# Where softmax is normalised in the sparse mixer of a two-layer hybrid decoder

## The chip, the cores and the metric

The kernel runs on one core of a Trainium2 chip. The metric is the device time of one execution in microseconds (us). The kernel before takes 1989.84 us, the median of three runs (1989.49, 1989.84 and 1992.78 us). A trace of one profiled execution stands beside these times.

A core has a matrix engine (TensorE, PE in the profile, with its weight loads as PEld), a vector engine (VectorE, DVE), a scalar engine (ScalarE, ACT), GpSimd (POOL) and a queue engine (SyncE, SP) that only starts transfers here. Each engine works through its own queue of instructions in order and waits on semaphores for the others. In this kernel the matrix engine writes its results to PSUM tiles and reads its operands from SBUF tiles.

## The reference

Each of two layers computes three token mixers from one input projection, merges them with per-channel gates, and adds a SwiGLU block. The sequence has 512 tokens, the model 1024 channels. The change is in the sparse mixer A, with 8 heads of 64 channels in 2 groups. It has three branches, each an attention of its own, and sums them with a sigmoid gate for each head, token and branch:

```
q_r = rope(q, pos)
s   = einsum(q_r, k_sel) * scale ;  p   = masked_softmax(s,   causal)     # selected blocks
s_w = einsum(q_r, k_win) * scale ;  p_w = masked_softmax(s_w, causal)     # sliding window
o_s = einsum(p, v_sel) ;  o_w = einsum(p_w, v_win)
o_c = einsum(masked_softmax(compressed scores), v_cmp)
g   = sigmoid(gate_logits)                      # 3 gates per head and token
o   = g[0] * o_c + g[1] * o_s + g[2] * o_w
```

With 512 tokens and 16 selected blocks of 64, and a window of 512, the selected and the window branch are both full causal attention, each with its own keys and values. Mixer B (multi-head latent attention, also 8 heads) runs through the same code without gates.

## The kernel before, in words

Each float32 product is made of three passes: an operand is split into a rounded part and a remainder (`split`, lines 98 to 100: the scalar engine copies, the vector engine or GpSimd subtracts), and `mm3` issues three matmuls.

The attention of a layer is a list of 24 jobs: 16 for mixer A (8 heads, and for each head branch b = 0, selected, and b = 1, window) and then 8 for mixer B. `attn` walks through slots g, three for each job, and in each slot issues one third of a stage for several jobs at once, so that the stages of different jobs overlap:

- `st_s` in slots 0 to 2 of a job: the score matmuls into a PSUM tile `pss` (two buffers, tag "s"); the masked row minimum `nm` on the vector engine (line 632); the exponential on the scalar engine into `P` in SBUF, with the row sum as a second result (line 635).
- `st_n`, four slots after a job's first: normalising, on the vector engine. For mixer A it takes the reciprocal of the row sums (line 642) and multiplies each of the job's four tiles `P` by the gate and by the reciprocal (line 644). For mixer B it only takes the reciprocal, for two heads at once (line 646).
- `st_t`, six slots after: `P` is transposed on the matrix engine (line 659) into a PSUM tile `pst` (three buffers, tag "t") and split into two tiles (line 100 on the scalar, line 101 on the vector engine).
- `st_v`, eight slots after: the product with the values into the PSUM tile `pso` (one buffer, tag "o", lines 672 and 673). For mixer A both branches of a head accumulate into the same tile: the first branch starts the accumulation (`first`), the second closes it (`last`). Only then is `pso` copied out: one half by the scalar engine (line 681), and the vector engine adds the other half to it (line 682). An even head fills the upper half of the tile `od`, an odd head the lower half.

After an odd head of mixer A the compressed branch is computed in one matmul (line 687) and added (line 688), and the sum is split into the operands of the projection that follows. After an odd head of mixer B the reciprocals are broadcast along 64 columns by the scalar engine (line 691), transposed on the matrix engine into a `pst` tile (line 696), and multiplied onto `od` (line 697). So mixer B normalises after the product with the values, on transposed outputs of two heads, and mixer A before it.

Between the stages `fill` issues matmuls of projections from a list (`fillers`) at a rate worked out from their due slots, and `step` issues small vector or GpSimd work from a list (`bg`: rotary embedding and norms of queries and keys). This order of issue is the program order. The tile framework then puts each engine's queue in an order of its own from dependencies, priorities and a model of durations; weight loads have a raised priority (`WPRI`). In the attention of both layers GpSimd makes the remainder of the weights (`wl`, line 101) and of the outputs (`oT`, `cq`), since `weng` is GpSimd there.

The tiles `od` and the broadcast `lb` come from the pool tag "e", with three buffers, which many other steps use too.

Of the kernel before, what the change touches and what calls it, by code (L numbers as in the profile page):

```python
# [12 lines left out]
F32R = mybir.dt.float32r  # L13
I32 = mybir.dt.int32
AF = mybir.ActivationFunctionType
# [48 lines left out]
class Builder:  # L64
    def __init__(self, ctx, tc, io, layers=L, dbg=None):
        self.tc, self.nc, self.io, self.layers = tc, tc.nc, io, layers
        self.dbg = dbg or {}
        nc = self.nc
        self.V, self.A, self.T = nc.vector, nc.scalar, nc.tensor
        pool = lambda n, b=1, **k: ctx.enter_context(tc.tile_pool(name=n, bufs=b, **k))  # L70
        self.cst, self.sb, self.sm = pool("cst"), pool("sb"), pool("sm", 2)
        self.psum = pool("psum", 1, space=PSUM)
        self.n = 0
        self.bufs = dict(wr=3, wh=4, wl=4, h=16, mg=8, oT=8, cq=10, qk=8, v=8, big=6, pt=5, P0=2, P1=2, P2=2, P3=3, e=3)
        self.pending = False
        self.pbufs = dict(mm=2, s=2, t=3, o=1)
        self.wide, self.turn = False, 0
        self.weng, self.debt, self.mid = None, 0.0, False

# [13 lines left out]
    def small(self, shape, tag, dt=F32):  # L93
        return self.sm.tile(shape, dt, tag=tag, name=self.nm(tag), bufs=2 if tag in ("vec", "nm", "l", "lp") else 1)
# [520 lines left out]
    def st_s(self, j, s):  # L615
        if s == 0:
            j.Pi = [self.pg(f"P{i}", F32, [128, 128 * i + 128]) for i in range(NT)]
            j.nm = self.small([128, NT], "nm")
            if j.cmp:
                j.l = self.small([128, NT], "l")  # L620
            else:
                if j.h % 2 == 0:
                    self.lp = self.small([128, 2, NT], "lp")
                j.lp = self.lp
                j.l = j.lp[:, j.h % 2]
# [12 lines left out]
    def st_n(self, j, part):  # L638
        V = self.V
        if j.cmp:  # L640
# [24 lines left out]
    def st_v(self, j, s):  # L665
        T = self.T
        if j.first and s == 0:
            self.o = self.ps("o")
        o = self.o
        for kt in ((0,), (1,), (2, 3))[s]:  # L670
            h, l_, m0, n = j.dst[kt]
            T.matmul(o[:, 512 - n:], j.V[kt], h[:, m0:m0 + n], start=j.first and kt == 0, stop=False)  # L672
            T.matmul(o[:, 512 - n:], j.V[kt], l_[:, m0:m0 + n], start=False, stop=j.last and kt == NT - 1)  # L673
        if s < 2:
            return
        if j.last:
            odd = j.h % 2
            if not odd:
                self.od = self.pg("e")
            r, s = (slice(64, 128), slice(0, 64)) if odd else (slice(0, 64), slice(64, 128))  # L680
            self.A.activation(self.od[r], o[s], AF.Copy)
            self.V.tensor_tensor(self.od[r], o[r], self.od[r], OP.add)
            if odd:
                if j.cmp:
                    pc = self.ps("t")
                    r = slice((j.h // 2 % 2) * 64, (j.h // 2 % 2) * 64 + 64)
                    T.matmul(pc, self.vbd[j.h // 4][r], self.PcT[r], start=True, stop=True)
                    self.V.tensor_tensor(self.od, pc, self.od, OP.add)
                else:
                    lb = self.pg("e")  # L690
                    self.A.activation(lb.rearrange("p (i h d) -> p i h d", i=NT, h=2),
                                      j.lp.rearrange("p h i -> p i h")[:, :, :, None].to_broadcast([128, NT, 2, 64]),
                                      AF.Copy)
                    pc = self.ps("t")
                    for i in range(NT):
                        T.transpose(pc[:, i * 128:i * 128 + 128], lb[:, i * 128:i * 128 + 128], self.ident)
                    self.V.tensor_tensor(self.od, pc, self.od, OP.mult)
                if j.cmp:
                    hi, lo = self.pg("oT", F32R), self.pg("oT", F32R)
                else:  # L700
                    hi, lo = self.pg("cq", F32R), self.pg("cq", F32R)
                self.split(hi, lo, self.od, self.weng)
                self.yo.append((hi, lo))
# [29 lines left out]
    def a_jobs(self, g):  # L733
        jobs = []
        for h in range(4 * g, 4 * g + 4):
            for b in range(2):
                j = Job()
                j.h, j.first, j.last, j.cmp = h, b == 0, b == 1, True

                def op(j=j, h=h, b=b):  # L740
                    k1, k2 = self.Kt[b]
                    q = self.Qt[h % 4]
                    j.gate = self.gth[:, :, h * 3 + 1 + b]
# [170 lines left out]
    def b_jobs(self):  # L914
        jobs = []
        for h in range(B_H):
            j = Job()
            j.h, j.first, j.last, j.cmp, j.gate = h, True, True, False, None
# [385 lines left out]
def build(d, layers=L, dbg=None):  # L1304
    nc = bacc.Bacc("TRN2", target_bir_lowering=False, num_devices=1)
# [18 lines left out]
```

## Time and profile before

| | |
|---|---|
| median of three runs | 1989.84 us (1989.49 to 1992.78) |
| span of the profiled execution | 1990.7 us; the page lists no longer time for it |
| PE busy | 1942.9 us, 98% |
| PEld busy | 1638.4 us, 82% |
| DVE busy | 1317.9 us, 66% |
| ACT busy | 996.6 us, 50% |
| POOL busy | 251.0 us, 13% |
| mean granted TensorE clock | 0.991 |

The jobs of mixer A run from about 115 to 312 us of the span in the first layer and from about 1100 to 1292 us in the second. Busy time is the time in which an engine had an instruction at work. The ends of matmuls are modelled, and neighbours overlap, so the start of the next matmul tells more of its real cost than its duration. A granted clock of 1.00 is 2.4 GHz and 0.50 is 1.2 GHz; a value between is a stretch with both.

### The profile page before, as it was taken

How to read it: one execution, taken by the hardware profiler on the slowest of the kernel's cores; microseconds unless marked ns; L12 is line 12 of the kernel's file. 1: busy time of each engine (PE TensorE's matmuls, PEld its weight loads, DVE VectorE, ACT ScalarE, POOL GpSimd, SP SyncE). 2: the span in 40 equal slices, each digit the busy share in tenths (PEclk: the TensorE clock that was granted, in tenths of full speed). 3: DMA queues.
4: the chain of work that ended last, by engine and by line, in shares of the span. 5: the costliest groups of instructions: out<-in, count | busy, mean ns of one | idle time of the engine just before them, and what ended most of it. 6: DMA issues, size and time to landing. Idle time of an engine off the chain costs nothing.

```text
span 1990.7 us, 26971 instructions
## 1 busy us (share of the span) xinstructions
PE 1942.9 (98%) x9472; PEld 1638.4 (82%) x9472; DVE 1317.9 (66%) x2783; ACT 996.6 (50%) x1937; POOL 251.0 (13%) x232
## 2 busy tenths in 40 slices
PE   9899999999999999999998899999999999999999
PEld 8878878888888888888888688888888888888887
DVE  8689998788545554455555999977884455534552
ACT  5456776687334332233344577767773343323331
POOL 0453442000000000000004535410000000000000
PEclk9898999999999999999999999999999999999999
DMA  5221111233333333333432111113333323333333
GB/s 155 76 68 30 38 33 42 89 93 101 111 122 101 95 96 97 99 95 98 130 113 87 48 37 47 33 47 98 96 102 116 122 95 96 95 97 99 96 102 99
DMA packets 100519, 173.94 MB, mean 87 GB/s; under 512 B 11936, under 2 KB 26144, under 8 KB 100384
## 3 DMA queue, kind: packets, MB, share of 16 engines
q1 hardware_dynamic: 100384, 172.22, 28.3%
q8 instruction: 74, 1.21, 0.3%
q14 instruction: 61, 0.50, 0.1%
HBM read 167.98 MB, written 4.19 MB: 86 GB/s over the span
## 4 chain that ended last, share of the span: by engine, by line
PE 79%; DVE 7%; ACT 2%; issue 1%; ACTq 0%; DVEq 0%
PE pst L113 10%; PE pst L115 10%; PE pst L114 10%; PE psmm L113 8%; PE psmm L114 8%; PE psmm L115 8%; PE pss L114 7%; PE pss L113 7%; PE pss L115 7%; PE pst L659 2%; DVE P L644 1%; DVE pss L632 1%; PE pso L672 1%; PE pso L673 1%; PE pst L543 1%
## 5 line engine op out<-in xcount | busy, mean ns | idle before, releaser
L100 ACT ACTIVATE wh<-wr 128x512 fp32r<-128x512 f32 (+3 forms) x640 | 387.7, 608 | 705.3 <-PE pst L114 261.3
L101 DVE TENSOR_TENSOR wl<-wr,wh 128x512 fp32r<-128x512 f32 (+2 forms) x526 | 355.0, 676 | 249.5 <-ACT wh L100 244.5
L101 POOL TENSOR_TENSOR wl<-wr,wh 128x512 fp32r<-128x512 f32 (+2 forms) x114 | 137.9, 1215 | 962.8 <-ACT wh L100 951.4
L113 PE MATMUL psmm<-h,wh 128*128 128x512 f32 x600 | 237.8, 396 | 1.4 <-ACT wh L100 1.0
L114 PE MATMUL psmm<-h,wh 128*128 128x512 f32 x600 | 235.6, 393 | 0.0
L115 PE MATMUL psmm<-h,wl 128*128 128x512 f32 x600 | 235.2, 392 | 0.0
L113 PE MATMUL pst<-h,wh 128*128 128x512 f32 x512 | 199.7, 390 | 0.0
L115 PE MATMUL pst<-h,wl 128*128 128x512 f32 x512 | 199.2, 389 | 0.0
L114 PE MATMUL pst<-h,wh 128*128 128x512 f32 x512 | 199.2, 389 | 0.0
L113 PE MATMUL pss<-h,wh 128*128 128x512 f32 x344 | 134.1, 390 | 0.0
L115 PE MATMUL pss<-h,wl 128*128 128x512 f32 x344 | 133.9, 389 | 0.0
L114 PE MATMUL pss<-h,wh 128*128 128x512 f32 x344 | 133.8, 389 | 0.0
L113 PEld LDWEIGHTS psmm<-h,wh 128*128 128x128 f32 x600 | 113.5, 189 | 23.7 <-ACT wh L100 1.3
L115 PEld LDWEIGHTS psmm<-h,wl 128*128 128x128 f32 x600 | 113.4, 189 | 23.6
L114 PEld LDWEIGHTS psmm<-h,wh 128*128 128x128 f32 x600 | 113.6, 189 | 20.9
L635 ACT ACTIVATE P<-pss,nm 128x512 f32<-128x512 f32 x192 | 100.1, 525 | 55.4 <-DVE nm L632 32.3
L113 PEld LDWEIGHTS pst<-h,wh 128*128 128x128 f32 x512 | 96.1, 188 | 20.2 <-ACT e L983 0.4
L115 PEld LDWEIGHTS pst<-h,wl 128*128 128x128 f32 x512 | 96.1, 188 | 20.0
L114 PEld LDWEIGHTS pst<-h,wh 128*128 128x128 f32 x512 | 96.1, 188 | 19.8
L632 DVE CUSTOM_DVE_ANT_0 pss<-pss,mask 128x512 f32<-128x512 f32 x192 | 93.9, 490 | 7.5 <-PE pss L115 6.4
L659 PE MATMUL pst<-ident,P 128*128 128x128 f32 x480 | 77.8, 277 | 9.0 <-DVE P L644 5.3
L659 PEld LDWEIGHTS pst<-ident,P 128*128 128x128 f32 x480 | 59.3, 143 | 25.3 <-issue 15.0
(419 smaller groups left out, 4316.3 us busy)
## 6 DMA issues: line engine op xcount, KB each, us to landing
wr<-w SPq DMA_DIRECT2D x240, 256.0 KB, 2.6
wr<-wfm SPq DMA_DIRECT2D x188, 256.0 KB, 2.7
wr<-wpc SPq DMA_DIRECT2D x32, 256.0 KB, 2.7
wr<-wo SPq DMA_DIRECT2D x32, 256.0 KB, 2.6
wr<-wb SPq DMA_DIRECT2D x32, 192.0 KB, 2.4
wr<-w SPq DMA_DIRECT2D x32, 192.0 KB, 2.3
mg<-xT SPq DMA_DIRECT2D x16, 256.0 KB, 2.8
wr<-wpa SPq DMA_DIRECT2D x16, 256.0 KB, 2.6
```

What stands on the lines that cost most here:

```text
L100: self.A.activation(hi, src, AF.Copy)
L101: (eng or self.V).tensor_tensor(lo, src, hi.bitcast(F32), OP.subtract)
L113: mm(ps, a[0], b[0], start=first, stop=False)
L114: mm(ps, a[0], b[1], start=False, stop=False)
L115: mm(ps, a[1], b[0], start=False, stop=last)
L543: self.T.transpose(ps[:w, i * 128:i * 128 + 128], src(i, slice(c0, c0 + w)), self.ident)
L632: self.V.tensor_tensor_reduce(p[:, :W], p[:, :W], self.mask[:, 512 - W:], 1.0, 3e38, OP.add, OP.min, j.nm[:, i:i + 1])
L635: self.A.activation(j.Pi[i], p[:, :128 * (i + 1)], AF.Exp, bias=j.nm[:, i:i + 1], scale=-1.0, accum_out=j.l[:, i:i + 1])
L644: V.tensor_scalar(j.Pi[i], j.Pi[i], j.gate[:, i:i + 1], j.l[:, i:i + 1], op0=OP.mult, op1=OP.mult)
L659: self.T.transpose(ps[:, c:c + 128], j.Pi[i][:, kt * 128:kt * 128 + 128], self.ident)
L672: T.matmul(o[:, 512 - n:], j.V[kt], h[:, m0:m0 + n], start=j.first and kt == 0, stop=False)
L673: T.matmul(o[:, 512 - n:], j.V[kt], l_[:, m0:m0 + n], start=False, stop=j.last and kt == NT - 1)
```

## The change

For mixer A the probabilities are no longer scaled. Each branch gets its own `pso` tile, from its start to its end, and is copied out by itself into a tile `od` of its own (tag "od", three buffers). After an odd head, for each branch, the reciprocals of both heads are multiplied by the gates (one product of 128x8), broadcast by the scalar engine, transposed on the matrix engine, and multiplied onto the branch's `od`, as mixer B did already. After the second branch GpSimd adds the two branches, and then the compressed branch is added as before. The row sums of two heads share a tile for each branch (`lp0`, `lp1`). The scratch space for descriptors of dynamic transfers is set to 1024, which leaves SBUF for the three new buffers.

```
-self.bufs = dict(..., P3=3, e=3)
+self.bufs = dict(..., P3=3, e=3, od=3)
...
 def st_n(self, j, part):
-    if j.cmp:
-        a = 2 - 2 * part
-        V.reciprocal(j.l[:, a:a + 2], j.l[:, a:a + 2])
-        for i in (a + 1, a):
-            V.tensor_scalar(j.Pi[i], j.Pi[i], j.gate[:, i:i + 1], j.l[:, i:i + 1], op0=OP.mult, op1=OP.mult)
-    elif j.h % 2 and part:
+    if j.h % 2 and part:
         V.reciprocal(j.lp, j.lp)
+        if j.cmp:
+            V.tensor_tensor(j.lp, j.lp, j.gate, OP.mult)
...
 def st_v(self, j, s):
-    if j.first and s == 0:
+    if s == 0:
         self.o = self.ps("o")
...
+    odd = j.h % 2
+    if not odd:
+        self.od[j.b] = self.pg("od")
+    od = self.od[j.b]
     r, s = (slice(64, 128), slice(0, 64)) if odd else (slice(0, 64), slice(64, 128))
+    self.A.activation(od[r], o[s], AF.Copy)
+    self.V.tensor_tensor(od[r], o[r], od[r], OP.add)
+    if not odd:
+        return
+    lb = self.pg("e")
+    self.A.activation(lb.rearrange(...), j.lp.rearrange(...).to_broadcast([128, NT, 2, 64]), AF.Copy)
+    pc = self.ps("t")
+    for i in range(NT):
+        T.transpose(pc[:, i * 128:i * 128 + 128], lb[:, i * 128:i * 128 + 128], self.ident)
+    self.V.tensor_tensor(od, pc, od, OP.mult)
+    if j.cmp and j.b == 0:
+        return
+    if j.cmp:
+        o0 = self.od[0]
+        self.weng.tensor_tensor(od, od, o0, OP.add)
+        pc = self.ps("t")
+        T.matmul(pc, self.vbd[j.h // 4][r], self.PcT[r], start=True, stop=True)
+        self.V.tensor_tensor(od, pc, od, OP.add)
...
-    nc = bacc.Bacc("TRN2", target_bir_lowering=False, num_devices=1)
+    nc = bacc.Bacc("TRN2", target_bir_lowering=False, num_devices=1, dynamic_dma_scratch_size=1024)
```

The whole program loses 128 scalings of `P` and 64 reciprocals of 128x2 on the vector engine. It gains there 16 reciprocals of 128x8, 16 products of 128x8, 16 additions of 64x512 and 16 products of 128x512; 64 transposes on the matrix engine; 16 copies of 64x512 and 16 broadcasts of 128x512 on the scalar engine; and 8 additions of 128x512 on GpSimd. No transfer is added or removed.

The first place is the vector engine's queue in the first layer, where the second and third jobs of mixer A stand; before, with `P` the probabilities, `l` the row sums and `gth` the gates:

```order
L604 TENSOR_TENSOR e_1517<-e_1517,cl_1546 128x16x31
L642 RECIPROCAL l_1498<-l_1498 128x2 x2
L101 TENSOR_TENSOR pt_1640<-pst_1641,pt_1639 128x384
L644 TENSOR_SCALAR P_1496<-P_1496,gth_830,l_1498 128x512
L644 TENSOR_SCALAR P_1495<-P_1495,gth_830,l_1498 128x384
L644 TENSOR_SCALAR P_1494<-P_1494,gth_830,l_1498 128x256
L644 TENSOR_SCALAR P_1493<-P_1493,gth_830,l_1498 128x128
L632 ISA pss_1647,nm_1610<-pss_1647,mask 128x384
L632 ISA nm_1610 128x1
```

The same place now, where `lp` are the row sums of two heads:

```order
L605 TENSOR_TENSOR e_1510<-e_1510,cl_1533 128x16x31
L102 TENSOR_TENSOR pt_1585<-pst_1586,pt_1584 128x512
L340 TENSOR_TENSOR mg_1609<-psmm_1497,rsb_469 128x512
L639 RECIPROCAL lp_1316<-lp_1316 128x8
L677 TENSOR_TENSOR od_1619<-pso_1581,od_1619 64x512
L641 TENSOR_TENSOR lp_1316<-lp_1316,gth_830 128x8
L102 TENSOR_TENSOR pt_1625<-pst_1626,pt_1624 128x384
L630 ISA pss_1632,nm_1597<-pss_1632,mask 128x384
L630 ISA nm_1597 128x1
```

The four scalings that stood between the split of a transpose (`pt`) and the next row minimum (`nm`) are gone; the copy of a branch out of `pso` and the two small operations on `lp` stand there.

The second place is the end of the second pair of heads in the first layer. On the vector engine before, where `e_2303` is the tile `od` of both branches:

```order
L821 TENSOR_REDUCE bss_2557<-e_2569 128x4
L158 SCALAR_TENSOR_TENSOR bkt_2477<-bkt_2477,bks_2435 128x8
L682 TENSOR_TENSOR e_2303<-pso_2409,e_2303 64x512
L159 SCALAR_TENSOR_TENSOR bky_2476<-bkt_2477,bky_2476 128x8
L644 TENSOR_SCALAR P_2421<-P_2421,gth_830,l_2426 128x128
L688 TENSOR_TENSOR e_2303<-pst_2582,e_2303 128x512
```

And now, where `od_2291` is the tile of the window branch:

```order
L820 TENSOR_REDUCE bss_2545<-e_2557 128x4
L630 ISA pss_2594,nm_2519<-pss_2594,mask 128x384
L630 ISA nm_2519 128x1
L677 TENSOR_TENSOR od_2291<-pso_2503,od_2291 64x512
L687 TENSOR_TENSOR od_2291<-pst_2572,od_2291 128x512
L696 TENSOR_TENSOR od_2291<-pst_2579,od_2291 128x512
L102 TENSOR_TENSOR pt_2587<-pst_2588,pt_2586 128x384
```

The addition of the compressed branch follows the copy out of `pso` almost directly in both; now the product with the transposed reciprocals stands between them. On GpSimd at the same end before, where `big_2139` is a key tile of mixer B:

```order
L882 TENSOR_TENSOR big_2139<-big_2139,bky_2476 128x8x64
L887 TENSOR_TENSOR big_2139<-kpe_831,bky_2476 128x8x32
L884 TENSOR_TENSOR big_2139<-big_2139,gB_182 128x8x64
L101 TENSOR_TENSOR oT_2586<-e_2303,oT_2585 128x512
L101 TENSOR_TENSOR wl_2736<-wr_2734,wh_2735 128x384
```

And on GpSimd now, where the key tile is `big_2126`:

```order
L881 TENSOR_TENSOR big_2126<-big_2126,bky_2464 128x8x64
L886 TENSOR_TENSOR big_2126<-kpe_831,bky_2464 128x8x32
L883 TENSOR_TENSOR big_2126<-big_2126,gB_182 128x8x64
L692 TENSOR_TENSOR od_2291<-od_2291,od_2082 128x512
L102 TENSOR_TENSOR oT_2583<-od_2291,oT_2582 128x512
```

The sum of the branches (line 692 of the changed kernel) stands on GpSimd between the product of line 687 and the addition of line 696 on the vector engine, and three other GpSimd operations stand ahead of it.

## Rows read from the trace of the kernel before

**Rows 1.** The page: busy time and share of the span by engine, instructions.
```profile
PE 1942.9 (98%) x9472; PEld 1638.4 (82%) x9472; DVE 1317.9 (66%) x2783; ACT 996.6 (50%) x1937; POOL 251.0 (13%) x232
```

**Rows 2.** Windows: length, busy by engine (instructions), granted clock, DMA share, GB/s.
```profile
115.00:312.00 197.00, 182.12 (x1060) 155.64 (x1059) 187.63 (x565) 136.76 (x361) 87.51 (x82) 0.97 0.12 37
1100.00:1292.00 192.00, 179.83 (x1068) 153.72 (x1067) 180.57 (x562) 137.47 (x358) 88.62 (x82) 0.99 0.14 41
```

**Rows 3.** Waits of PE, 115 to 312 us: total us, times, longest us.
```profile
PE pss L747 <- ACT P L635: 6.8, 8, 1.4
PE pst L659 <- DVE P L644: 2.6, 2, 2.4
PE pst L659 <- DVE l L642: 1.9, 1, 1.9
```

**Rows 4.** Waits of PE, 1100 to 1292 us.
```profile
PE pss L747 <- ACT P L635: 3.8, 5, 1.3
PE pst L659 <- DVE P L644: 2.7, 1, 2.7
PE pst L659 <- DVE bbckvt L157: 1.8, 1, 1.8
```

**Rows 5.** Timeline of PE: start, length, instruction, idle before it and releaser.
```profile
154.34 0.63 PE L659 MATMUL pst<-ident,P 128*128 128x128 f32 x4 [2.43 <-DVE P L644]
266.69 0.52 PE L659 MATMUL pst<-ident,P 128*128 128x128 f32 x3 [1.86 <-DVE l L642]
1137.95 1.09 PE L659 MATMUL pst<-ident,P 128*128 128x128 f32 x4 [2.70 <-DVE P L644]
```

**Rows 6.** Windows just behind those three waits.
```profile
155.00:165.00 10.00, 10.00 (x37) 8.96 (x37) 8.34 (x29) 3.59 (x11) 6.05 (x6) 0.50 0.04 15
267.00:271.00 4.00, 4.00 (x20) 3.49 (x19) 3.99 (x12) 2.61 (x7) 3.94 (x6) 0.57 0.01 4
1138.00:1141.40 3.40, 3.40 (x11) 2.86 (x12) 3.40 (x16) 2.37 (x7) 0.00 (x0) 0.52 0.29 99
```

**Rows 7.** Timeline of DVE, one scaling alone and four in a row.
```profile
237.41 0.48 DVE L644 TENSOR_SCALAR P<-P,gth,l 128x384 f32<-128x384 f32 x1
...
1132.88 4.92 DVE L644 TENSOR_SCALAR P<-P,gth,l 128x512 f32<-128x512 f32 x4
```

**Rows 8.** Timeline of POOL beside those four.
```profile
1132.29 2.37 POOL L531 TENSOR_TENSOR big<-big,cosa 128x768 f32<-128x768 f32 x1
1134.62 2.78 POOL L101 TENSOR_TENSOR wl<-wr,wh 128x512 fp32r<-128x512 f32 x2
```

**Rows 9.** Groups by line, DVE: busy us, mean ns, idle before and releasers.
```profile
L644 DVE TENSOR_SCALAR P<-P,gth,l 128x512 f32<-128x512 f32 (+3 forms) x128 | 73.5, 599 | 0.4
L682 DVE TENSOR_TENSOR e<-pso,e 64x512 f32<-64x512 f32 x32 | 21.9, 686 | 5.4 <-ACT e L681 5.2
L642 DVE RECIPROCAL l<-l 128x2 f32<-128x2 f32 x64 | 9.3, 153 | 0.7 <-ACT P L635 0.7
L697 DVE TENSOR_TENSOR e<-pst,e 128x512 f32<-128x512 f32 x8 | 5.5, 689 | 0.6
```

**Rows 10.** One line, DVE: shortest, median and longest ns.
```profile
L602 DVE TENSOR_TENSOR cl<-gth,cl x4: 163/764/903, 146.8 to 1195.6; 128x16 f32<-128x16 f32 x4
L646 DVE RECIPROCAL lp<-lp x8: 192/202/203, 285.3 to 1323.2; 128x8 f32<-128x8 f32 x8
```

**Rows 11.** The chain of waits at the end of mixer A: start, length, what.
```profile
306.53 0.44 PE pst L696 x4
```

**Rows 12.** Groups by line, ACT and POOL.
```profile
L681 ACT ACTIVATE e<-pso 64x512 f32<-64x512 f32 x32 | 19.0, 592 | 15.7 <-PE pso L673 14.4 <-DVE bss L821 0.9
L691 ACT ACTIVATE e<-lp 128x512 f32<-128x512 f32 x8 | 5.0, 629 | 0.0
L101 POOL TENSOR_TENSOR oT<-e,oT 128x512 fp32r<-128x512 f32 x8 | 10.3, 1286 | 15.9 <-ACT oT L100 11.7 <-PE psmm L115 4.3
```

**Rows 13.** Timeline of PE: the last product of one job and the next job's first.
```profile
212.25 0.28 PE L673 MATMUL pso<-z,v 128*128 128x256 f32 x1
218.30 0.39 PE L672 MATMUL pso<-pt,v 128*128 128x512 f32 x1
```

More of the change, by code (lines that the diff above doesn't have):

```diff
@@ L78, in __init__ @@
         self.weng, self.debt, self.mid = None, 0.0, False
+        self.lp, self.od = {}, {}
     def nm(self, t):
@@ L93, in small @@
     def small(self, shape, tag, dt=F32):
-        return self.sm.tile(shape, dt, tag=tag, name=self.nm(tag), bufs=2 if tag in ("vec", "nm", "l", "lp") else 1)
+        return self.sm.tile(shape, dt, tag=tag, name=self.nm(tag), bufs=2 if tag in ("vec", "nm", "lp0", "lp1") else 1)
     def const(self, shape, name, dt=F32):
@@ L618, in st_s @@
             j.nm = self.small([128, NT], "nm")
-            if j.cmp:
[L620 to L625, printed above, removed]
+            if j.h % 2 == 0:
+                self.lp[j.b] = self.small([128, 2, NT], f"lp{j.b}")
+            j.lp = self.lp[j.b]
+            j.l = j.lp[:, j.h % 2]
         ps = self.ps("s")
@@ L671, in st_v @@
             h, l_, m0, n = j.dst[kt]
-            T.matmul(o[:, 512 - n:], j.V[kt], h[:, m0:m0 + n], start=j.first and kt == 0, stop=False)
-            T.matmul(o[:, 512 - n:], j.V[kt], l_[:, m0:m0 + n], start=False, stop=j.last and kt == NT - 1)
+            T.matmul(o[:, 512 - n:], j.V[kt], h[:, m0:m0 + n], start=kt == 0, stop=False)
+            T.matmul(o[:, 512 - n:], j.V[kt], l_[:, m0:m0 + n], start=False, stop=kt == NT - 1)
         if s < 2:
             return
[L676 to L703, printed above, removed]
@@ new lines, in st_v @@
+        pc = self.ps("t")
[8 more added lines that the diff above has]
+            pc = self.ps("t")
+            r = slice((j.h // 2 % 2) * 64, (j.h // 2 % 2) * 64 + 64)
+            T.matmul(pc, self.vbd[j.h // 4][r], self.PcT[r], start=True, stop=True)
+            self.V.tensor_tensor(od, pc, od, OP.add)
+            hi, lo = self.pg("oT", F32R), self.pg("oT", F32R)
+        else:
+            hi, lo = self.pg("cq", F32R), self.pg("cq", F32R)
@@ L705, in attn @@
+        self.split(hi, lo, od, self.weng)
+        self.yo.append((hi, lo))
     def attn(self, jobs, hooks):
@@ L737, in a_jobs @@
                 j = Job()
-                j.h, j.first, j.last, j.cmp = h, b == 0, b == 1, True
+                j.h, j.b, j.cmp = h, b, True
                 def op(j=j, h=h, b=b):
@@ L742, in op @@
                     q = self.Qt[h % 4]
-                    j.gate = self.gth[:, :, h * 3 + 1 + b]
+                    e = h - h % 2
+                    j.gate = self.gth.rearrange("p i (h b) -> p h b i", b=3)[:, e:e + 2, 1 + b]
                     j.V = [self.Va[kt][:, g * 2 + b, :] for kt in range(NT)]
@@ L917, in b_jobs @@
             j = Job()
-            j.h, j.first, j.last, j.cmp, j.gate = h, True, True, False, None
+            j.h, j.b, j.cmp = h, 0, False
             j.open = lambda: None
```

7 lines of the change are left out of this document (5 added, 2 removed).

## The prediction

> **What bounds the kernel now.** I read the page first: the matrix engine is busy for 98% of the span, and no other engine comes near it [rows 1]. By that row alone a change that adds matrix work and removes vector work should lose. The average hides two stretches, though, so I read the windows next. In the jobs of mixer A, 197 us in the first layer and 192 us in the second, the matrix engine is busy for 182.12 and 179.83 us, and the vector engine for 187.63 and 180.57 us [rows 2]. There the two are equally full, and the matrix engine stands idle for 14.9 + 12.2 = 27.1 us. This is the only place that the change touches, and what it is worth is decided by who waits for whom there.
>
> The waits of the matrix engine answer that. In four places the transposes of P wait for the vector engine to normalise: 2.6 us for the scaling and 1.9 us for the reciprocal in the first layer, 2.7 us in the second [rows 3, 4], 7.2 us in all. The largest other item is the score matmul that waits for the exponential to free its PSUM tile, 6.8 and 3.8 us [rows 3, 4]. The exponential itself follows the row minimum on the vector engine, so these are the vector engine's backlog one step further. With the 1.8 us behind another vector chain the backlog makes 6.8 + 3.8 + 1.8 = 12.4 us. The rest of the 27.1 us, some 7.5 us, is small waits for other things.
>
> A second loss lies behind the three long waits of 2.43, 1.86 and 2.70 us [rows 5]. Right after each of them the granted clock is at or near half: 0.50 for 10.00 us, 0.57 for 4.00 us, 0.52 for 3.40 us [rows 6], which is the level of 1.2 GHz with a little of 2.4 GHz at an edge. The matrix engine is busy throughout these, so they lose 10.00 x 0.50 + 4.00 x 0.43 + 3.40 x 0.48 = 5.0 + 1.7 + 1.6 = 8.3 us.
>
> **The change part by part.**
>
> Removed from the vector engine: 128 scalings, 73.5 us, and 64 reciprocals, 9.3 us [rows 9], together 82.8 us, half in each layer. Nearly all of it lies in the two windows.
>
> Added there: 16 copies out of PSUM at 0.686 us, 11.0 us, and 16 products with a PSUM operand at 0.689 us, 11.0 us [rows 9]; 16 reciprocals of 128x8 at 0.20 us, 3.2 us [rows 10]; and 16 products of the reciprocals with the gates. The last have no row of their own. The nearest is a product of 128x16 with the same gates, between 0.16 and 0.90 us long [rows 10]; I take its median of about 0.76 us less what its half size may save, 0.65 us, and 10.4 us in all, with ends of 2.6 and 14.4 us. Sum 35.6 us. So the vector engine falls from 368.2 to about 321 us in 389 us, from 95% to 82%.
>
> What these small products cost depends on GpSimd. A scaling alone takes 0.48 us for 128x384; four in a row took 4.92 us [rows 7] while GpSimd had 2.37 and 2.78 us of work beside them [rows 8]. So the scalings are dear where the two engines meet, and that is where the longest wait of the matrix engine comes from: it ends at 1137.95 us [rows 5], with the fourth scaling. The Trainium skill (SBUF — State Buffer, "Who interferes with whom") says that a vector instruction in a two-port mode, or one with two SBUF inputs against a GpSimd instruction that reads SBUF, and a GpSimd instruction exclude each other for a whole instruction. The trace agrees with it in the 4.92 us. By that rule the added product of sums and gates, which has both inputs in SBUF, may still wait for a whole GpSimd operation each time, while the new additions and products with a PSUM input may not; with the 1.286 us of a GpSimd operation added to all 16 it would be about 23 us instead of 10.4, and the vector engine at 86% instead of 82%.
>
> The matrix engine gains 64 transposes in 16 groups of four. The same group exists in mixer B and takes 0.44 us on the chain [rows 11]: 16 x 0.44 = 7.0 us. This lies on the path wherever the matrix engine is the limit, and I count it in full (its lower end is 0, if all of it falls into idle time).
>
> The scalar engine gains 16 copies at 0.592 and 16 broadcasts at 0.629 us [rows 12], 19.5 us, and goes from 274.2 to 293.7 of 389 us, 75%. GpSimd gains 8 additions of about 1.29 us [rows 12], 10.3 us beside 176 us. Both are covered by their idle time, as far as nobody stands behind them.
>
> What returns: the 7.2 us of direct waits go, since the transposes then need only the exponentials of six slots earlier. With these gaps gone I expect the clock to stay up, 8.3 us. Of the 12.4 us of backlog I take half, 6.2 us, because 82% is not empty and the row minimum still stands in the same queue (ends 0 and 12.4 us). Sum 21.7 us.
>
> New waits: three kinds. First, pso has one buffer, and the second branch's first product must now wait until the first branch is copied out. Between the last product of a job and the first of the next lie 218.30 - 212.25 = 6.05 us [rows 13], and the copy and addition need 0.59 + 0.69 us [rows 9, 12] behind whatever is queued; behind a late product stand the fillers and the transposes on the matrix engine. I price it at nothing, covered by these 6 us. Second, the scalar engine's broadcast stands in one place directly behind a copy that waits for the product with the values, and the four transposes wait for it; 0.59 + 0.63 = 1.22 us at worst, at 16 places 19.5 us, at best 0, because in mixer B the same group of transposes never shows an idle gap. Third, the vector engine's last addition waits for GpSimd's sum of the branches; behind it wait the next splits and row minima. Its worst is 1.29 us eight times, 10.3 us on the vector engine, of which its free 18% hides most. For the last two together I take 3.0 us, near their lower ends (0 and 29.8 us).
>
> The edit of the descriptor scratch and the new pool tag change no transfer; their cost is 0. That `od` leaves the three buffers of tag "e" can only help; I count nothing.
>
> Sum: -21.7 + 7.0 + 3.0 = -11.7 us against the profiled span of 1990.7 us, which gives 1979.0 us. The page gives no time around that span, and the median of the runs is 0.9 us less than it, so I forecast 1978 us for the median.
>
> **The rivals.**
>
> *All idle time goes.* With the vector engine at 82% the matrix engine never waits: -27.1 - 8.3 + 7.0 = -28.4 us, 1961.4 us by the median. For it speaks that nearly every long wait ends with the vector engine; against it, that the waits for chains of short steps (rotary embedding, statistics) are latency, not load.
>
> *The gain is spent on the transposes.* Only the direct waits go, the half clock returns behind other gaps, and the backlog is set by the exponentials themselves: -7.2 + 7.0 = -0.2 us, 1989.6 us, no change. For it speaks that the scalar engine gets fuller by 19.5 us just where the score matmuls wait for it; against it, that it has a quarter of its time free.
>
> *The vector engine stops behind GpSimd (slower).* At the end of each pair of heads the product of line 687, GpSimd's sum and the addition of line 696 follow each other. In the second pair nothing stands between the two on the vector engine, and three GpSimd operations stand ahead of the sum. One stop is then 1.29 us for the sum and the rest of those in front, some 2.5 us. If eight such stops land on the matrix engine, and the gap of 2.5 us puts the clock down as the three gaps of 1.86 to 2.70 us did [rows 5, 6], then only the 7.2 us return: 1989.8 - 7.2 + 7.0 + 8 x 2.5 = 2009.6 us; with four of them 1999.6 us. It decides from the point where eight stops eat the other gains, (11.7 + 3.0) / 8 = 1.8 us each. Against this rival speaks that in five other places of the new order other vector work stands in between, and that the free 18% lies right behind each stop.
>
> *The change does not take the normalising off the path,* because the transposes then wait for the exponentials instead. The reciprocals that stand ahead of the scalings never waited for long, 0.7 us in all [rows 9], so the exponentials were there; I give it no chance of its own and count it with the second rival.
>
> **How the numbers follow.** The forecast with its own range, 1968 to 1985 us, gets 0.54; all idle time gone, below 1968 us, 0.14; gain spent, 1986 to 1994 us, 0.17; slower, 0.15. What three runs can tell from no change is about 0.2%, 4 us, so faster means below 1985.9 and slower above 1993.8 us: faster 0.68, same 0.17, slower 0.15. The range for 8 in 10 takes in the full recovery nearly to its end and the case without change: 1963 to 1995 us.
>
> **What would show it.** In the profile after, the transposes of P should show no wait for normalising, and the three windows of half clock should be gone; the vector engine should be at 80 to 86% in mixer A, and the matrix engine's idle time there at 10 to 16 us. The four transposes of the broadcast should show no idle time before them, or little. I am wrong if the matrix engine waits for `od` or behind the scalar engine's broadcast, if the vector engine's addition behind GpSimd's sum shows stops of 1.8 us or more, or if the score matmuls wait for the exponentials as long as before with the vector engine no longer full.

## The result, and the profile after

The changed kernel takes 2004.28 us, the median of four runs (2001.92 to 2006.57), against 1990.72 us for the kernel before in the same runs: a ratio of 1.0067 with a 95% interval of 1.0054 to 1.0081. It is 13.6 us slower, where the forecast was 1978 us with a range up to 1995 us. The profiled execution has a span of 2003.0 us; its run took 2004.86 us. "Against before" is always against the median of the kernel before in the same comparison.

The page after, as in [rows 1]:

```profile
PE 1948.8 (97%) x9536; PEld 1644.5 (82%) x9536; DVE 1281.5 (64%) x2655; ACT 1017.2 (51%) x1969; POOL 258.7 (13%) x240
```

VectorE has 36.4 us less to do and ScalarE 20.6 us more. The windows of mixer A come next, as [rows 2] and [rows 6]; the second stretch is 12 us longer, since it ends later.

```profile
115.00:312.00 197.00, 180.24 (x1087) 154.86 (x1086) 163.80 (x501) 146.71 (x377) 90.38 (x85) 0.98 0.12 37
155.00:165.00 10.00, 10.00 (x66) 8.89 (x65) 9.36 (x44) 7.43 (x19) 1.29 (x1) 1.00 0.15 52
1100.00:1304.00 204.00, 186.42 (x1100) 159.73 (x1099) 166.26 (x496) 147.74 (x376) 92.47 (x86) 0.97 0.12 39
1250.00:1256.00 6.00, 5.99 (x21) 5.23 (x21) 3.14 (x8) 4.35 (x10) 1.20 (x1) 0.52 0.01 5
```

VectorE is at 83% and 82% there, the share that was forecast. Yet the matrix engine now stands idle for 16.8 + 17.6 = 34.4 us, more than the 27.1 us of before. The half clock of [rows 6] at 155 us is gone; a new one stands at 1250 us, and another, at 145 us, comes up below with the return. The waits of the matrix engine in the second layer, as in [rows 4] (total us, times, longest us):

```profile
PE pso L667 <- ACT z L101: 4.7, 1, 4.7
PE pst L686 <- ACT e L681: 2.4, 2, 1.9
PE pss L746 <- ACT P L633: 2.3, 4, 1.2
PE psmm L114 <- ACT pt L101: 1.8, 1, 1.8
PE pso L667 <- DVE od L677: 1.5, 1, 1.5
```

The wait for normalising is gone and the one for the exponentials fell from 3.8 to 2.3 us. New on top is one wait of a value product for the tile z (the last split of the transposed P). The line of VectorE's addition in the changed kernel says where it comes from: shortest, median and longest ns, then what it waited for and who waited for it.

```profile
L696 DVE TENSOR_TENSOR od<-pst,od x8: 690/692/692, 177.5 to 1281.9; 128x512 f32<-128x512 f32 x8
...
  POOL od L692: 16.1, 8
...
  ACT oT L101: 11.5, 8
```

All eight additions stopped behind GpSimd's sum, 16.1 us in all, and ScalarE's copy for the split of `oT` stopped behind them for 11.5 us. The longest stop is at the third pair of heads in the second layer. GpSimd's timeline there (start, length, instruction, idle before it):

```profile
1238.33 2.90 POOL L833 TENSOR_TENSOR big<-big,bqy 128x768 f32<-128x768 f32 x2 [2.65 <-DVE bqy L160]
1241.19 0.46 POOL L836 TENSOR_TENSOR e<-big,qn 128x128 f32<-128x128 f32 x1
...
1245.07 0.72 POOL L842 TENSOR_TENSOR big<-big,e 128x256 f32<-128x256 f32 x1
1245.74 1.26 POOL L692 TENSOR_TENSOR od<-od,od 128x512 f32<-128x512 f32 x1
```

VectorE's:

```profile
1239.89 0.69 DVE L687 TENSOR_TENSOR od<-pst,od 128x512 f32<-128x512 f32 x1
1240.49 0.56 DVE L630 CUSTOM_DVE_ANT_0 pss<-pss,mask 128x384 f32<-128x384 f32 x1
1240.97 0.14 DVE L630 DVE_READ_ACCUMULATOR2_ANT nm<- 128x1 f32 x1
1240.97 0.55 DVE L102 TENSOR_TENSOR pt<-pst,pt 128x384 fp32r<-128x384 f32 x1
1247.04 0.69 DVE L696 TENSOR_TENSOR od<-pst,od 128x512 f32<-128x512 f32 x1 [5.52 <-POOL od L692]
```

ScalarE's:

```profile
1247.76 0.63 ACT L101 ACTIVATE oT<-od 128x512 fp32r<-128x512 f32 x1 [5.89 <-DVE od L696]
1248.36 0.63 ACT L925 ACTIVATE mg<-mg 128x512 f32<-128x512 f32 x1
1248.90 0.47 ACT L101 ACTIVATE z<-pst 128x384 fp32r<-128x384 f32 x1
```

And the matrix engine's:

```profile
1244.40 0.33 PE L668 MATMUL pso<-pt,v 128*128 128x384 f32 x1
1249.42 0.58 PE L667 MATMUL pso<-z,v 128*128 128x256 f32 x1 [4.69 <-ACT z L101]
```

Read them in this order. The product (line 687) is done at 1240.58 us, but ten operations of mixer B's queries (lines 833 to 842), begun at 1238.33 us, stand ahead of the sum in GpSimd's queue, so the sum starts at 1245.74 us. VectorE's addition waits for it, ScalarE's copy of `oT` waits for that, and the copy of z, which has nothing to do with either, stands two places behind on ScalarE. The matrix engine waits 4.69 us for it and then runs at a granted clock of 0.52 for 6 us, near the level of 1.2 GHz, which loses another 2.9 us. The Trainium skill (Perfetto Trace Analysis, "Tensor Engine Instruction (MATMUL, LD_WEIGHTS)") says that ScalarE, VectorE and GpSimd are strict FIFO; these three queues agree.

The next table follows that along a layer: start of the first transposes of P of a job (jobs counted from 0), in us against the kernel before, from the matrix engine's timelines of the profiled executions. The first three columns are jobs of the first layer, the last four of the second.

| kernel | 3 | 13 | 19 | 3 | 12 | 14 | 19 |
|---|---|---|---|---|---|---|---|
| changed | -6.6 | -3.2 | -0.7 | -5.4 | +0.6 | +7.9 | +12.3 |
| changed, all sums on VectorE | -6.8 | -4.7 | -6.0 | -10.8 | -5.0 | -5.6 | -4.3 |
| before, without normalising | -4.6 | -2.9 | -7.0 | -13.7 | -13.1 | -12.0 | -12.4 |

The changed kernel gains some 6 us by job 3 of the first layer and loses it by job 19; in the second layer the jump from job 12 to job 14 is mostly the stop just shown.

### The profile page after: what moved, and what is told of

The parts are those of the page before. It is cut to its first block, busy times and chain, and to the rows that moved or that the text cites. A ratio compares the mean times of both kernels' runs of the same rounds, so it can differ in the third digit from the quotient of the medians.

```text
span 2003.0 us, 26994 instructions
## 1 busy us (share of the span) xinstructions
PE 1948.8 (97%) x9536; PEld 1644.5 (82%) x9536; DVE 1281.5 (64%) x2655; ACT 1017.2 (51%) x1969; POOL 258.7 (13%) x240
## 4 chain that ended last, share of the span: by engine, by line
PE 81%; DVE 10%; ACT 4%; POOL 3%; issue 2%; DMA 1%; SPq 0%; POOLq 0%; DVEq 0%; ACTq 0%
PE pst L114 10%; PE pst L115 10%; PE pst L116 10%; PE psmm L114 8%; PE psmm L116 8%; PE psmm L115 8%; PE pss L114 7%; PE pss L115 7%; PE pss L116 7%; PE pst L654 1%; ACT P L633 1%; DVE pss L630 1%; PE pso L667 1%; PE pso L668 1%; DVE qk L550 1%
## 5 line engine op out<-in xcount | busy, mean ns | idle before, releaser
L114 PEld LDWEIGHTS pss<-h,wh 128*128 128x128 f32 x344 | 64.6, 188 | 13.4
```

Of the source, the lines that this page charges most:

```text
L114: mm(ps, a[0], b[0], start=first, stop=False)
```

## The experiments

Theory 1: the loss is the stops behind GpSimd's sum. Theory 2: it is the added work, with transposes, broadcasts and copies.

**sum_on_vector.** The edit of the changed kernel:

```
-            self.weng.tensor_tensor(od, od, o0, OP.add)
+            self.V.tensor_tensor(od, od, o0, OP.add)
```

> The changed kernel with one word changed: the sum of the two branches (line 692) is made on VectorE instead of GpSimd, 8 times. Theory 1 (the loss is VectorE standing behind GpSimd's sum, and ScalarE's half of the split behind that): the four pairs lose their stops, of which 5.52 us at 1247 us and 3.99 us at 259 us were the long ones; the jump of 6.6 us at the 14th job of the second layer and of some 3.7 us at jobs 11 to 13 of the first go, 10.3 us, and with the smaller stops up to 13 us: 1991 to 1994 us. Theory 2 (the loss is the added work, 64 transposes, 16 broadcasts, 16 copies and products): no change or a little worse, 2001 to 2006 us, since VectorE gets 8 operations more.

Measured: 1989.39 us against 1991.22, ratio 0.999 (0.9982 to 0.9999). One operation on another engine gives back 15.4 us of difference to the kernel before (+13.6 to -1.8). Theory 2 falls as the main cause. The time lies 1.6 us below theory 1's lower end, and the 15.4 us are near the 16.1 us that the eight stops last. That is so for the total only: third_pair_on_vector shows that the two long stops cost more than they last and the six short ones less.

**sum_last** asks which of the stopped engines matters.

```
-            o0 = self.od[0]
-            self.weng.tensor_tensor(od, od, o0, OP.add)
...
             self.V.tensor_tensor(od, pc, od, OP.add)
+            self.weng.tensor_tensor(od, od, self.od[0], OP.add)
```

> The changed kernel with two statements in the other order: VectorE adds the compressed branch first, and GpSimd's sum comes last, straight before the split. VectorE never stands behind the sum then; ScalarE's half of the split still does, and GpSimd's half follows on its own engine. Theory 1a (it is VectorE's stop that counts): nearly as good as with the sum on VectorE, 1991 to 1996 us. Theory 1b (it is ScalarE's stop that counts, since the exponentials and the copies of the split stand behind it): little is won, 2000 to 2005 us, with stops of 3 to 6 us of ScalarE in front of the split of oT. Theory 2 (added work): 2001 to 2006 us.

Measured: 2000.95 us, ratio 1.0046 (1.0034 to 1.0059), +9.7 against before. VectorE's addition no longer stops, but ScalarE does, and so does VectorE behind it. Its timelines at the third pair, ScalarE:

```profile
1246.73 0.63 ACT L101 ACTIVATE oT<-od 128x512 fp32r<-128x512 f32 x1 [5.17 <-POOL od L695]
```

and VectorE:

```profile
1243.04 0.14 DVE L630 DVE_READ_ACCUMULATOR2_ANT nm<- 128x1 f32 x1
1248.29 0.56 DVE L102 TENSOR_TENSOR z<-pst,z 128x384 fp32r<-128x384 f32 x1 [5.10 <-ACT z L101]
```

By itself this looks like theory 1b, ScalarE's stop; the opposite run (split_on_gpsimd) shows that it isn't.

**before_no_normalising**, the most that the removal can return: in `st_n` of the kernel before, for mixer A,

```
-            a = 2 - 2 * part
-            V.reciprocal(j.l[:, a:a + 2], j.l[:, a:a + 2])
-            for i in (a + 1, a):
-                V.tensor_scalar(j.Pi[i], j.Pi[i], j.gate[:, i:i + 1], j.l[:, i:i + 1], op0=OP.mult, op1=OP.mult)
+            return
```

> The kernel before without the reciprocals and scalings of P in mixer A (its output is therefore not normalised there), nothing put in their place: what taking 82.8 us from VectorE can return at most. If the forecast's terms hold (7.2 us of direct waits, 8.3 us of half clock, half to all of 12.4 us of backlog): 1962.8 to 1969.0 us. If VectorE's load was not what held the stretch: 1983 to 1991 us.

Measured: 1976.68 us, ratio 0.992 (0.9905 to 0.9936), -14.5 us. It lies between the two expectations: the term of 21.7 us was too large, with nothing put in place of the scalings at all. Where the rest went is shown further down.

**after_no_gate_product**: broadcast, transposes and product run only for mixer B.

```
-        lb = self.pg("e")
-        self.A.activation(lb.rearrange(...), j.lp.rearrange(...), AF.Copy)
...
-        self.V.tensor_tensor(od, pc, od, OP.mult)
+        if not j.cmp:
+            lb = self.pg("e")
+            self.A.activation(lb.rearrange(...), j.lp.rearrange(...), AF.Copy)
...
+            self.V.tensor_tensor(od, pc, od, OP.mult)
```

> The changed kernel without the 16 broadcasts, 64 transposes and 16 products of mixer A (its sums and gates are not multiplied on, the rest stands): the price of this chain. Theory 1: the matrix engine gets its 7.0 us back and VectorE 11 us, GpSimd's sum keeps its queue and its stops: 1993 to 1998 us. Theory 2 (added work is the loss): 1985 us or less, since then this chain costs 19 us or more.

Measured: 1996.44 us, ratio 1.0023 (1.0013 to 1.0033), +5.2 against before, where the changed kernel has +13.6. The chain costs some 8 us there, near the estimate of the forecast.

**third_pair_on_vector** asks whether every sum is dear or only those behind a queue.

```
+            (self.V if j.h % 8 == 5 else self.weng).tensor_tensor(od, od, o0, OP.add)
```

> The changed kernel with the sum of the branches on VectorE for the third pair of heads alone, so for 2 of the 8 sums; six stay on GpSimd. Theory 1 (what counts is the queue ahead on GpSimd, mixer B's operations of line 833 and the following, and it is long only at the third pair, where the two stops of 3.99 and 5.52 us were): most of the 14.9 us that came back with all eight on VectorE, 10 to 12 us, 1992 to 1995 us. Rival (each sum on GpSimd costs about the same, 14.9 / 8 = 1.9 us): 3.7 us, 2000 to 2001 us.

Measured: 1991.8 us, ratio 1.0004 (0.9995 to 1.0013), +1.1. Moving two sums of eight brings 12.5 of the 15.4 us, where their stops had lasted 9.5 us; the other six stops last 6.6 us and cost the remaining 2.9 us. The value products of that job take z without idle time at 1238.87 us here (1249.42 us in the changed kernel), and the work behind them, which ran at 0.52 there, has the full clock:

```profile
1236.00:1242.00 6.00, 6.00 (x36) 5.25 (x35) 5.29 (x15) 4.65 (x14) 5.92 (x10) 1.00 0.00 0
```

**qpost_on_vector** leaves all sums on GpSimd and takes the queue away from ahead of them.

```
-        V, E = self.V, self.peng
+        V, E = self.V, self.V if hf else self.peng
```

> The changed kernel with the ten operations of mixer B's second half of queries (line 833 and the following, 7.2 us of GpSimd's queue ahead of the third sum in each layer) on VectorE instead of GpSimd; all sums stay on GpSimd. Theory 1 (the queue ahead made the sum late, the sum itself is cheap): the two long stops shrink to some 1.4 us, as at the other pairs; 1992 us as with the third pair's sum on VectorE, plus what VectorE's ten added operations cost, at most some 4 us a layer: 1992 to 2000 us. Rival (the stop stays, since VectorE itself is late with the product in front of the sum): 2002 to 2010 us.

Measured: 1996.37 us, ratio 1.0029 (1.0018 to 1.0041), +5.9. Behind the same sums on the same engine VectorE now stops for 6.8 us instead of 16.1, the line of VectorE's addition again:

```profile
  POOL od L692: 6.8, 7
  ACT oT L101: 2.9, 7
```

So the queue made the sum late. The 4.8 us above the run before it are put down to VectorE's ten added operations a layer (the two of line 833 take 0.96 us each there, as median); that share was not measured by itself.

**idle_sum_on_gpsimd** adds GpSimd's load without a waiting engine.

```
+            self.weng.tensor_tensor(self.pg("sc"), o0, o0, OP.add)
             self.V.tensor_tensor(od, od, o0, OP.add)
```

> The kernel with all sums on VectorE, and beside each a GpSimd addition of the same size (the first branch's output to itself) into a tile that nobody reads: GpSimd's load and its queue are as in the changed kernel, but no engine waits for it. Theory 1 (the wait is the loss, not the load): 1989 to 1991 us. Rival (GpSimd's eight operations slow VectorE's small work beside them, or delay the splits of oT behind them on GpSimd): 1994 to 2004 us.

Measured: 1990.63 us, ratio 1.0001 (0.9992 to 1.001), -0.1; with one input tile an addition takes 1.04 us instead of 1.28. GpSimd's load costs some 1.7 us beside sum_on_vector, a small part of the 15.4 us, so the loss is the wait.

**sum_on_vector_no_gate_product**: sum_on_vector and the edit of after_no_gate_product together.

> The kernel with all sums on VectorE, and without the 16 broadcasts, 64 transposes and 16 products of mixer A (sums and gates are not multiplied on): the price of this chain where nothing stands behind GpSimd. Theory 1 (the transposes are paid in full, 7.0 us, and little more): 1981.5 to 1982.5 us, as 7.8 us came back in the kernel with the stops. Rival a (the transposes fall into idle time there): 1986 to 1989 us. Rival b (VectorE's products and ScalarE's broadcasts cost as much again): 1977 to 1979 us, at the level of the kernel before without its normalising, 1976.7 us.

Measured: 1980.51 us, ratio 0.9948 (0.9934 to 0.9961), -10.2. The chain of broadcast, transposes and product costs 8.4 us (from -1.8 to -10.2), a little above theory 1's 7 to 8; what is left of the added work (a copy and an addition for each branch, the sums, the small products) costs 4.3 us (from -14.5 to -10.2).

**split_on_gpsimd**, the opposite of sum_last: VectorE stops, ScalarE doesn't.

```
+        if j.cmp:
+            self.weng.tensor_copy(hi, od)
+            self.weng.tensor_tensor(lo, od, hi.bitcast(F32), OP.subtract)
+        else:
+            self.split(hi, lo, od, self.weng)
```

> The changed kernel with the rounded half of the split of mixer A's outputs copied on GpSimd instead of ScalarE (8 times); the sum stays on GpSimd and VectorE's addition stays behind it. So VectorE stops and ScalarE doesn't, the opposite of the run with the sum last (2000.95 us, ScalarE stops and VectorE doesn't). Theory 1b (ScalarE's stop is the loss): 1990 to 1994 us. Theory 1c (either stop is enough to lose most of it, since both engines stand ahead of the transposed P on its way to the value products): 1998 to 2004 us, with stops of VectorE of 4 to 6 us in the third pair.

Measured: 2003.12 us, ratio 1.0065 (1.0053 to 1.0078), +12.7. Theory 1c holds and 1b falls. ScalarE has made its half of z at 1241.29 us; VectorE stops, and its half comes at 1248.10. VectorE and then the matrix engine in this run:

```profile
1246.56 0.69 DVE L696 TENSOR_TENSOR od<-pst,od 128x512 f32<-128x512 f32 x1 [5.52 <-POOL od L692]
...
1248.10 0.55 DVE L102 TENSOR_TENSOR z<-pst,z 128x384 fp32r<-128x384 f32 x1
```

```profile
1248.71 0.58 PE L668 MATMUL pso<-z,v 128*128 128x256 f32 x1 [4.31 <-DVE z L102]
```

The value product needs both halves of z, one from each engine. A stop of either is enough.

**early_broadcast** (on sum_on_vector): ScalarE's broadcast is issued in `st_v` at the first step of an odd head, not after the last.

```
         if s == 0:
             self.o = self.ps("o")
+            if j.h % 2:
+                lb = j.lb = self.pg("e")
+                self.A.activation(lb.rearrange(...), j.lp.rearrange(...), AF.Copy)
...
+        lb = j.lb
```

> The kernel with all sums on VectorE, and ScalarE's broadcast of the gate over the sum issued at the first step of the value products of an odd head instead of after the last, so ahead of the copy that waits for these products. Theory 1: the transposes' waits for the broadcast go, 1.1 us in the first layer and 2.1 us in the second: 1986 to 1988 us. Rival (the broadcast then holds one of three buffers that mixer B's small work uses too, and delays the copies of the splits on ScalarE): 1990 to 1995 us.

Measured: 1986.89 us, ratio 0.9982 (0.9973 to 0.9991), -3.8. **broadcast_with_reciprocal** moves the same three lines from `st_v` to the end of `st_n`, behind line 641.

> The kernel with all sums on VectorE and the early broadcast, issued still earlier: directly behind the product of reciprocals and gates (in mixer B behind its reciprocals). Theory 1: the one wait of the transposes for it that is left, 1.7 us in the second layer, goes: 1984 to 1987 us. Rival (it stands in ScalarE's queue ahead of exponentials that are due earlier, or holds a buffer of tag e too long): 1987 to 1992 us.

Measured: 1986.24 us, ratio 0.9981 (0.9973 to 0.999), -4.2: the same within the intervals.

**gpsimd_does_all** (on early_broadcast): the edits of sum_last and split_on_gpsimd together, so nobody waits.

> The kernel with the early broadcast; the sum is on GpSimd again, but last, and both halves of the split follow it on GpSimd, so neither VectorE nor ScalarE ever waits for GpSimd there, and each has 8 operations less. Theory 1 (only the stops cost, wherever the sum is made): 1984 to 1988 us, like the early broadcast with the sum on VectorE (1986.9 us). Rival (GpSimd gets 8 x 2.5 us more, and its splits of the weights come late for the matrix engine): 1990 to 1998 us.

Measured: 1984.95 us, ratio 0.9973 (0.9964 to 0.9982), -5.5. Each of the two edits alone returned 1 to 4 us of the changed kernel's +13.6; together, and with the early broadcast (worth 2.0 us on sum_on_vector), they return 19.1 and leave a kernel faster than before, with GpSimd's sum in it. The two without the early broadcast were not run. The line of that sum in this run, with nobody under "who waited":

```profile
L697 POOL TENSOR_TENSOR od<-od,od x8: 1284/1290/1297, 177.5 to 1263.8; 128x512 f32<-128x512 f32 x8
...
who waited for it (us, times):
```

**no_normalising_e4** goes after the missing 7.2 us of the forecast's return. In before_no_normalising VectorE comes early to a tile of tag e, and stops; its half of z comes late, and the value product waits. The two lines of that run's timeline, then the windows:

```profile
142.68 0.81 DVE L784 TENSOR_TENSOR e<-kpe 128x128 f32<-128x128 f32 x1 [5.17 <-POOL big L537]
...
146.48 0.39 PE L670 MATMUL pso<-z,v 128*128 128x256 f32 x1 [3.16 <-DVE z L101]
```

```profile
145.00:155.00 10.00, 8.00 (x28) 6.58 (x29) 8.89 (x31) 4.44 (x13) 2.74 (x3) 0.66 0.19 54
245.00:255.00 10.00, 8.07 (x27) 5.35 (x26) 8.13 (x22) 4.21 (x11) 7.86 (x11) 0.72 0.27 79
```

The clock lost 3.4 + 2.8 = 6.2 us here, most of the 8.3 us that the forecast had expected back. The edit, with the change's smaller descriptor scratch to make room:

```
-        self.bufs = dict(..., P3=3, e=3)
+        self.bufs = dict(..., P3=3, e=4)
```

> The kernel before without its normalising in mixer A, with a fourth buffer of tag e (and the smaller descriptor scratch of the change, which makes the room). Theory (the gain stopped at 14.5 us because VectorE, being early, runs into a tile that GpSimd still reads, 5.2 us, which makes the value products wait 3.2 us for z and drops the clock to 0.66 for 10 us, 3.4 us): about 6.6 us come back, 1969 to 1972 us. Rival (other waits take its place, the ones behind the exponentials of P above all, and the clock falls behind those): 1974.5 to 1978 us.

Measured: 1968.65 us, ratio 0.9886 (0.9872 to 0.9899), -23.1. At the first place this run has no idle time and no half clock. At the second the same work now stands 8 us earlier; the wait for z is as long as before (1.93 us there, 1.90 us here), and the half clock behind it is shorter. The first window, the value product, and the window behind it:

```profile
145.00:155.00 10.00, 10.00 (x65) 8.71 (x64) 9.15 (x25) 5.64 (x15) 9.65 (x10) 1.00 0.27 79
...
240.82 0.38 PE L670 MATMUL pso<-z,v 128*128 128x256 f32 x1 [1.90 <-DVE z L101]
...
242.00:246.00 4.00, 4.00 (x13) 3.11 (x12) 3.20 (x7) 2.52 (x6) 4.00 (x6) 0.57 0.02 7
```

So in the profiled executions the first place returns 7.0 us (the first transposes of P of job 2 start at 147.77 us for 155.26, those of job 1 at 139.94 for 140.39) and the second 2.2 us, for which the shorter half clock accounts in the main. **before_e4** is the control.

> The kernel before with a fourth buffer of tag e and the smaller descriptor scratch, nothing else: the control. Its trace shows no stop of VectorE at this tile, since VectorE comes to it some 12 us later behind the scalings. Theory: no change, 1989 to 1992.5 us. Rival (a buffer more helps whatever the rest is, as GpSimd waits 4.9 us for such a tile): 1983 to 1987 us.

Measured: 1992.27 us, ratio 1.0005 (0.9996 to 1.0013). The buffer is worth nothing where VectorE is late anyway, so the 8.6 us (from -14.5 to -23.1) belong to the removal of the scalings; the stop had kept most of them.

**gpsimd_does_all_e4** puts the fourth buffer into gpsimd_does_all.

> The kernel with sum and split on GpSimd and the early broadcast, with a fourth buffer of tag e. It shows the same stop of 5.2 us, the wait for z of 3.2 us, and the clock at 0.83 for 10 us, 1.7 us. Theory: 4.9 us come back, 1979 to 1982 us. Rival (other waits take its place): 1983.5 to 1986 us.

Measured: 1983.45 us, ratio 0.9964 (0.995 to 0.9977), -8.3. The stop is gone and the profiled span is 5.3 us shorter (1977.9 for 1983.2), but the profiled run is the fastest of five that spread from 1979.69 to 1986.35 us, the median lies 1.5 us above theory's range, and the interval overlaps that without the buffer. What the buffer brings here stays open. **gpsimd_all_early_e4** has the broadcast of broadcast_with_reciprocal as well.

> As the run with sum and split on GpSimd and a fourth buffer of tag e, but with the broadcast straight behind the product of reciprocals and gates. Theory: the waits of the transposes for the broadcast, 0.9 us, go as well: 1978.5 to 1981.5 us. Rival (the broadcast holds its tile so long that the fourth buffer is used up by it, and the stop stays): 1983.5 to 1986 us.

Measured: 1983.56 us, ratio 0.9958 (0.9945 to 0.997), -8.2. This is 2.1 us above theory's range, and no better than without the earlier broadcast. These two are the fastest complete versions, 0.4% below the kernel before.

## Why the prediction was wrong, point by point

The forecast's sum was -21.7 + 7.0 + 3.0 = -11.7 us. The runs give, as differences to the kernel before, -14.5 for the removal, +8.4 for the chain on transposed outputs, +4.3 for the other added work, and +15.4 for the waits behind the sum: +13.6 us. Each is a difference between two runs, so the split holds for this order of steps. Of the 25.3 us between the two, 12.4 are the waits, 7.2 the return, 4.3 the work that was priced at nothing, and 1.4 the chain.

*The step that failed* is the third of the new waits: "Its worst is 1.29 us eight times, 10.3 us on the vector engine, of which its free 18% hides most." Both halves were wrong. The worst case of a wait for an engine is its queue ahead plus the operation, here 7.4 us of mixer B's queries (1238.33 to 1245.74 us) and then 1.26. Of the queue 5.16 us were left when the product was done; with the sum, and less the 0.94 us for which VectorE had other work, that is the stop of 5.52 us. It was 3.99 us at the other third pair and 0.4 to 1.5 us elsewhere. Free time of 18% hid more than half of the short stops (2.9 us paid for 6.6) and nothing of the long ones (12.5 us paid for 9.5), since the split of z behind the stopped engines is due at once; the free time lies after it. The forecast's third rival had this mechanism, with a stop of 2.5 us and a deciding point of 1.8 us each; the eight stops averaged 2.0 us, above that point. It counted three GpSimd operations ahead at the second pair and took five other places to be safer because VectorE has other work in between. At the third pair that work covers 0.94 us and the queue is 7.4 us long. The forecast counted ScalarE's new work, but not that it would stop in turn behind VectorE's addition.

*The return of 21.7 us* was right as the worth of taking the scalings away, and wrong as the worth of this removal in this program: 14.5 us as it stands, 23.1 us with a fourth buffer. The direct waits went, as the waits after show. But "with these gaps gone I expect the clock to stay up" missed that an engine that comes earlier runs into the next thing, a tile that GpSimd still reads. The changed kernel has the same stop; VectorE's wait from 120 to 312 us, then the window:

```profile
DVE e L786 <- POOL big L538: 5.2, 1, 5.2
...
145.00:150.00 5.00, 3.60 (x12) 2.95 (x13) 4.96 (x16) 2.23 (x8) 2.92 (x3) 0.66 0.20 56
```

It stands as well in before_no_normalising, sum_on_vector and sum_on_vector_no_gate_product, so the return of 14.5 us contains it, and the differences between these runs have it on both sides. What it costs the changed kernel isn't shown: in broadcast_with_reciprocal it shrank to 0.6 us, and the time stayed within the intervals of early_broadcast, which has it in full.

In the kernel before that stop doesn't show, because VectorE reaches the tile only at 155.4 us, 12.7 us after the stop's end in before_no_normalising.

*The transposes* were sized well: 7.0 us forecast, 8.4 with broadcast and product. Their waits for ScalarE's broadcast, 3.5 us in mixer A after, were inside the bounds; issuing it earlier brought 2.0 us.

*Copies and additions for each branch* were priced at nothing, hidden by idle time. With the sums and the small products they cost 4.3 us. A single cause was not separated; the value product that waits 1.5 us for `od` in the waits after is one part:

```profile
1135.09 0.50 PE L667 MATMUL pso<-pt,v 128*128 128x512 f32 x1 [1.47 <-DVE od L677]
```

The forecast held it covered by the 6.05 us of [rows 13]. Here 6.01 us lie between the two products and did not cover it, and 6.05 us was one instance: in the kernel before the distance in mixer A goes down to 1.27 us.

*The vector engine's load* came out as a share, 83 and 82% against a forecast of 82%, but in part by luck. Its busy time there fell by 38.1 us (from 368.2 to 330.1) where the forecast had 47.2, although the small product took 0.17 us (median) and not 0.65; the share fits because the second stretch is 12 us longer. Why the fall was smaller was not followed up. That the share came out, and the time still rose, is the lesson: idle share said nothing about who stands behind whom. The prediction's sentences on what the two engines cost each other hung on that product. In sum_on_vector VectorE's sum, with both inputs in SBUF, took 0.68 us at the shortest, 0.74 us as median and 1.78 us at the longest; the longest started at 281.93 us, 0.04 us behind a GpSimd subtraction of 1.28 us. The Trainium skill (SBUF — State Buffer, "Who interferes with whom") says that such a VectorE instruction contends with a GpSimd instruction that reads SBUF; these times agree.

## What to carry to other kernels

When a result is moved to a lightly loaded engine, price the wait for it by what stands ahead of it in that engine's queue at that moment, and then list what stands behind the waiting instruction on each engine in the chain; the load of either engine answers neither question. If two engines each make one half of an operand, freeing one of them alone returns little (3.8 and 0.9 us of 15.4 here): let nobody wait (gpsimd_does_all), or make the result on the engine that needs it (sum_on_vector). When work is removed from an engine, ask which buffer or result it will now reach too early.

## What the runs showed of the hardware

After a single gap of 4.69 us (the changed kernel) the granted clock was 0.52 for 6 us, so the stop and the clock behind it cost 4.7 + 2.9 us. In before_no_normalising it was 0.66 from 145 to 155 us, with a gap of 3.16 us that ends at 146.48 us; in no_normalising_e4, without that gap, it was 1.00 there.

The length of the gap alone does not say how long the half clock lasts. Behind gaps of nearly the same length it was 0.53 over 7 us (1.93 us, before_no_normalising) and 0.57 over 4 us (1.90 us, no_normalising_e4, in the line shown with that run). The window of before_no_normalising:

```profile
249.00:256.00 7.00, 7.00 (x21) 4.68 (x21) 4.26 (x11) 3.78 (x10) 6.33 (x9) 0.53 0.08 28
```

GpSimd rounded a 128x512 tile in 0.61 us, in gpsimd_does_all and split_on_gpsimd, half of the 1.28 us that it takes for an addition or subtraction of that size with two inputs.
